# A 31-tap convolution over grid rows: from VectorE taps to TensorE matrices, with relayouts through DRAM

## The chip, the core and the metric

The kernel runs on one core of a Trainium2 chip. The metric is device time of one execution in microseconds. Engines are named as in the profile: PE is TensorE (PEld its weight loads), DVE VectorE, ACT ScalarE, POOL GpSimd, SP the queue that issues most DMAs.

## What is computed

One layer of a hybrid backbone: 1024 latent tokens on a grid of 16 rows of 64 columns, 256 context tokens, width 1024. An input projection gives a DeltaNet head group (queries, keys, values, gates) and a Conformer channel group of 512 channels; both are put together, projected, and followed by a mixture of experts. The change concerns the channel group alone:

```
y = a * sigmoid(b)                    # a, b: 512 columns each of the input projection
y = conv_grid_columns(y, w) + dw_b    # depthwise, 31 taps along the 16 grid rows, zero padding
y = silu(layernorm(y, ln_g, ln_b))    # over the 512 channels
```

For a channel, column and output row `r` the sum is over input rows `r + t - 15`: with 16 rows every output row sees all 16 input rows, each with its own tap.

## The kernel before

The work is emitted through a framework that builds each engine's instruction order at build time: it simulates the program, takes what is ready by the order of the source (and first what stands under `first()`), and puts in the semaphores. At run time each engine and each DMA queue goes through its fixed order and waits where an operand is missing. Tiles live in pools; a pool has a fixed place and size in every partition, pools opened with `side="right"` are stacked from the other end and grow downwards, and a tile laid over one of a closed pool waits for the last reader of that tile (`reuse_waits="tile"`).

The stages that matter here, all on feature-major tiles (128 channels by tokens):

- `cf_project(j, hf)` (lines 368 to 376) projects block `j` of 128 channels for one half of the tokens: 24 matmuls each for b and a in split fp32 (`fm`, L320), tanh on ScalarE (L374), and on VectorE `YG[j] = (tanh + 1) * a` (L376). The missing factor 0.5 is in the tap weights `cfw` (L400). `YG` has two buffers.
- `load_cf` and `load_in` stream the weights: SP loads (L302), ScalarE and GpSimd split into two parts (L293, L294), two buffers each. `mod_block` (L256 to L268) computes modulation vectors from `w_mod`.
- The convolution (loop at L411): ScalarE starts `ycv[:, j]` with the middle tap and the bias (L421), and VectorE adds the other 30 taps, one instruction each (L427), each on the tokens that the shift of `64 * (t - 15)` leaves.
- The layernorm (L458 to L488) in two halves of 512 tokens: column sums on TensorE (`channel_mean`, L462 and L466), copied by ScalarE (L464), subtraction, squares, reciprocal root, product, silu on VectorE and ScalarE (L473 to L487), and a store to `hc_d` in DRAM (L488).
- `qkv_block` projects a block of 128 channels of the heads: `fm` into PSUM tag "a" (four banks), ScalarE copies to `cx` and `cc` (L557, L565), `conv7` on VectorE (L548), transposes (L573), stores to `kv_d` (L584). Four key blocks come first, then the key norms (L662), then value blocks with `prep1` and `base_inverse` (L694 to L736, with DMAs through `wt_d`, `bounce` and `rep`), then query blocks.
- `conv_out(hf)` (L593 on) reads `hc_d` back in tiles `hcs` of 128 tokens (L602), splits them and multiplies with `w_out` (L612), adds `x` (`hx`, L604, L613) and stores to `yo_d`.

The places of the pools in the program of before, in bytes of each partition: `cf` (YG, modulation weights) 27,104 to 76,896; `gbase` 63,968 to 74,400; `cv` (cx 74,400 to 82,648, then cc, ot, sq, ac) 74,400 to 101,152; `ln` (ycv first, 16,384 bytes, then rv, sql and small ones) 101,536 to 124,896; `win` (weights and activations) 124,896 to 229,344. `cf` and `ln` live together; `cv` and `gbase` are opened after both are closed in the source, but run beside the layernorm where nothing lies under them.

Of the kernel before, what the change touches and what calls it, by code (L numbers as in the profile page):

```python
# [8 lines left out]
F32 = mybir.dt.float32  # L9
# [140 lines left out]
def hybrid_kernel(tc, a, out):  # L150
# [19 lines left out]
    def csl(c):  # L170
        return slice(c * 128, (c + 1) * 128)
# [72 lines left out]
    def vcol(n, i=0, k=1):  # L244
        return vec[:, pos[n] + i:pos[n] + i + k]
# [122 lines left out]
    def cf_project(j, hf):  # L368
        wb, wa = wab[j]
        if hf == 0:  # L370
            YG[j] = cfp.tile([128, 1024], F32, name="yg", bufs=2)
        pb = fm(wb, 1 + hf)
        tb = cfp.tile([128, 512], F32, name="tb", bufs=2)
        S.activation(tb, pb, AF.Tanh, scale=0.5)  # L374
        pa = fm(wa, 1 + hf)
        V.scalar_tensor_tensor(YG[j][:, hf * 512:(hf + 1) * 512], tb, 1.0, pa, op0=OP.add, op1=OP.mult)  # L376
# [20 lines left out]
    PE.transpose(pt[:, 0:84], cr, ident[:84, :84])  # L397
    PE.transpose(pt[:, 128:252], fr, ident[:124, :124])
    V.tensor_copy(cnv, pt[:, 0:84])
    V.tensor_scalar(cfw, pt[:, 128:252], 0.5, None, op0=OP.mult)  # L400
    load_x(0, 2)
    stats(0, 2)
    scale_shift('mcx', 'g_mix', 8, 0, 1)
# [1 line left out]
    st_pre.close()  # L405


    st_l = ExitStack()
    lnp = st_l.enter_context(tc.tile_pool(name="ln", bufs=1, side="right", reuse_waits="tile"))
    ycv = lnp.tile([128, 4, 1024], F32, name="ycv")  # L410
    for j in range(4):  # L411
        if j:
            for hf in range(2):
                cf_project(j, hf)
        if j < 3:
            load_cf(j + 1)
        for n in (4 + 2 * j, 5 + 2 * j):
            mod_block(n)
        yg = YG[j]
        yc = ycv[:, j, :]  # L420
        S.activation(yc, yg, AF.Identity, scale=cfw[:, 60 + j:61 + j], bias=vcol('dw_b', j))  # L421
        for t in range(31):
            if t == 15:
                continue
            d = (t - 15) * 64
            lo, hi = max(0, -d), min(1024, 1024 - d)
            V.scalar_tensor_tensor(yc[:, lo:hi], yg[:, lo + d:hi + d], cfw[:, t * 4 + j:t * 4 + j + 1], yc[:, lo:hi],  # L427
                                   op0=OP.mult, op1=OP.add)

    scale_shift('mf', 'g_ffn', 32, 24, 0)  # L430
    gt_d = dp.tile([32, 128], F32, name="gt_d")
# [23 lines left out]
    hc_d = dp.tile([128, 4, 1024], F32, name="hc_d")  # L455


    def channel_mean(get):  # L458

        ps = bank("b")  # L460
        for j in range(4):
            PE.matmul(ps[32 * j:32 * j + 32, :], ones[:, :32], get(j), start=True, stop=True, tile_position=(0, 32 * j))  # L462
        sm = lnp.tile([128, 512], F32, name="sm", tag="rv", bufs=1)
        S.activation(sm, ps, AF.Copy)  # L464
        ps = bank("b")
        PE.matmul(ps, onm, sm, start=True, stop=True)  # L466
        return ps

    for hf in range(2):
        sl = slice(hf * 512, (hf + 1) * 512)  # L470
        pm = channel_mean(lambda j: ycv[:, j, sl])
        for j in range(4):
            V.tensor_sub(ycv[:, j, sl], ycv[:, j, sl], pm)  # L473

        def square(j):
            sq = lnp.tile([128, 512], F32, name="sql", bufs=2)
            S.activation(sq, ycv[:, j, sl], AF.Square)
            return sq

        pv = channel_mean(square)  # L480
        rv = lnp.tile([128, 512], F32, name="rv", bufs=1)
        V.tensor_scalar(rv, pv, EPS, None, op0=OP.add)
        S.activation(rv, rv, AF.Sqrt)
        V.reciprocal(rv, rv)
        for j in range(4):
            V.tensor_mul(ycv[:, j, sl], ycv[:, j, sl], rv)
            S.activation(ycv[:, j, sl], ycv[:, j, sl], AF.Silu, scale=vcol('ln_g', j), bias=vcol('ln_b', j))  # L487
            SY.dma_start(hc_d[:, j, sl], ycv[:, j, sl])  # L488
# [104 lines left out]
    def conv_out(hf):  # L593

        hs_ = slice(hf * 512, (hf + 1) * 512)
        gb = cvp.tile([128, 512], F32, name="gb", tag="sq", bufs=1)
        SY.dma_start(gb, gt_d[4 * hf:4 * hf + 4].rearrange("k p -> (k p)").partition_broadcast(128))
        wt = [load_w(w['w_out'].rearrange("(k p) n -> p k n", p=128)[:, 4 + 2 * i:6 + 2 * i, hs_], 2, gb)
              for i in range(2)]
        for t in range(8):  # L600
            hs = cvp.tile([128, 4, 128], F32, name="hcs", tag="ot", bufs=2)
            SY.dma_start(hs, hc_d[:, :, csl(t)])  # L602
            hx = prp.tile([128, 512], F32, name="hx", tag=("rf", "rb")[t % 2])
            SY.dma_start(hx, x[csl(t), hs_])  # L604
            hr = cvp.tile([128, 2, 4, 128], F32R, name="hcr", tag="ac", bufs=2)
            hch, hcl = split(hs, hr[:, 0], hr[:, 1], (V, G)[t % 2])
            yield
            ps = bank("a")
            for k in range(4):
                wh, wl = wt[k // 2]  # L610
                for i, (l, r) in enumerate(((hch, wh), (hcl, wh), (hch, wl))):
                    PE.matmul(ps, l[:, k, :], r[:, k % 2, :], start=(k == 0 and i == 0), stop=(k == 3 and i == 2))  # L612
            V.tensor_tensor(hx, ps, hx, op=OP.add)  # L613
            SY.dma_start(yo_d[csl(t), hs_], hx)
# [1218 lines left out]
```

## Time and profile before

| | us |
|---|---|
| median of 3 runs | 1735.57 (1733.73 to 1736.39) |
| the profiled execution | 1741.28 |
| its span, first to last instruction | 1739.6 |
| PE busy in the span | 1575.7 |
| DVE busy | 1001.3 |
| ACT busy | 494.5 |
| POOL busy | 537.5 |

A busy share over the span says little, since the stages differ: up to some 563 us the projections, convolutions and preparations run, then the scans, then the experts. An instruction that ends late matters only if another one waits for it; so the views by stage, in order of time and of the waits are read together. The mean granted clock of TensorE over the span was 0.964.

### The profile page before, as it was taken

What the parts mean: (1) busy time and instruction counts of PE and PEld (TensorE: products, weight loads), DVE (VectorE), ACT (ScalarE), POOL (GpSimd) and SP (SyncE); (2) the same over time, 40 slices, a digit from 0 to 9 for tenths busy, and PEclk for the clock granted to TensorE, in tenths of its full rate; (3) what the DMA queues carried; (4) which work ended last, traced back from release to release, by engine and by line L of the source; (5) the groups of instructions that cost most, each with busy time, mean ns of one, the idle gap of its engine ahead of it and who ended that gap; (6) DMA issues with size and microseconds to landing.
All of it is one profiled execution on the core that took longest, in us unless ns stands there. A gap on an engine that the chain in (4) does not pass through costs nothing. (4 is left out here: it accounts for less than half of the span.)

```text
span 1739.6 us, 23353 instructions
## 1 busy us (share of the span) xinstructions
PE 1575.7 (91%) x8348; PEld 924.7 (53%) x8348; DVE 1001.3 (58%) x2236; ACT 494.5 (28%) x1071; POOL 537.5 (31%) x486
## 2 busy tenths in 40 slices
PE   5989998876869899798999999999999999999990
PEld 1557667764647899687544434344444344433440
DVE  2488989889671886878712444444444444443425
ACT  4531266534122212444212121212121111121212
POOL 2321214543212677732011232323232222232212
PEclk8999999998889999899999999999999999999995
DMA  9455123434643334766358999999999999999956
GB/s 318 152 175 176 37 65 94 121 106 124 167 145 127 109 104 154 233 220 218 120 223 304 340 345 342 329 366 335 334 380 381 342 337 331 344 383 370 354 137 232
DMA packets 151112, 412.12 MB, mean 237 GB/s; under 512 B 19383, under 2 KB 66900, under 8 KB 125396
## 3 DMA queue, kind: packets, MB, share of 16 engines
q1 hardware_dynamic: 129994, 334.62, 53.3%
q0 software_dynamic: 18288, 67.05, 15.2%
q10 hardware_dynamic: 2714, 8.95, 1.3%
q8 instruction: 66, 1.08, 0.3%
q14 instruction: 50, 0.41, 0.1%
HBM read 339.48 MB, written 71.43 MB: 236 GB/s over the span
## 5 line engine op out<-in xcount | busy, mean ns | idle before, releaser
L1353 PE MATMUL gu<-wg,hg 128*32 128x512 f32 (+2 forms) x1968 | 463.2, 599 | 0.7 <-ACT hg L1604 0.7
L1629 DVE SCALAR_TENSOR_TENSOR ob<-dn,wc,gt2b 128x512 f32<-128x512 f32 x124 | 93.0, 750 | 366.0 <-PE dn L1373 366.0
L1638 POOL DMA_INDIRECT acc<-ob,ic x89 | 134.6, 1513 | 530.3 <-DVE st L1563 460.1
L1353 PEld LDWEIGHTS gu<-wg,hg 128*32 128x32 f32 (+2 forms) x1968 | 148.4, 137 | 203.2 <-issue 159.2
L1373 PE MATMUL dn<-wd,sg 128*32 128x512 f32 (+2 forms) x984 | 226.8, 597 | 0.5 <-ACT sg L1364 0.5
L1604 ACT ACTIVATE hg<-xt,mf 128x128 f32<-128x128 f32 x248 | 93.4, 456 | 376.4 <-PE xt L1598 375.9
L320 PE MATMUL a<-hTh,whi 128*128 128x512 f32 (+1 forms) x448 | 171.5, 383 | 3.7 <-ACT cx L557 3.7
L320 PE MATMUL a<-hTh,wlo 128*128 128x512 f32 (+1 forms) x448 | 170.3, 380 | 0.0
L320 PE MATMUL a<-hTl,whi 128*128 128x512 f32 (+1 forms) x448 | 170.3, 380 | 0.0
L1373 PEld LDWEIGHTS dn<-wd,sg 128*32 128x32 f32 (+2 forms) x984 | 77.8, 137 | 143.5 <-issue 142.7
L294 POOL TENSOR_TENSOR wlo<-wst,whi 128x512 fp32r<-128x512 f32 x56 | 82.3, 1487 | 214.3 <-ACT whi L293 209.7
L1602 DVE TENSOR_SCALAR hg<-xt,mf 128x128 f32<-128x128 f32 x248 | 84.3, 401 | 50.4 <-DMA acc<-hg 50.4
L427 DVE SCALAR_TENSOR_TENSOR ycv<-yg,cfw,ycv 128x64 f32<-128x64 f32 (+14 forms) x120 | 101.3, 844 | 6.1 <-ACT ycv L421 2.9
L320 PEld LDWEIGHTS a<-hTh,whi 128*128 128x128 f32 x448 | 84.8, 189 | 30.2 <-issue 9.9
L320 PEld LDWEIGHTS a<-hTh,wlo 128*128 128x128 f32 x448 | 85.0, 190 | 18.7 <-issue 3.4
L320 PEld LDWEIGHTS a<-hTl,whi 128*128 128x128 f32 x448 | 84.9, 189 | 18.0 <-issue 3.0
L1588 POOL DMA_INDIRECT xg<-xn_d,ig x62 | 74.1, 1195 | 64.9 <-DVE st L1583 28.3
L1552 DVE TENSOR_TENSOR oh<-posl 128x1024 bf16<-128x1024 f32 (+3 forms) x89 | 77.6, 897 | 0.0
L1598 PE MATMUL xt<-ident,xg 128*128 128x128 f32 x496 | 70.3, 285 | 0.0
L293 ACT ACTIVATE whi<-wst 128x512 fp32r<-128x512 f32 x56 | 33.0, 624 | 107.0 <-PE a L320 66.2
L1358 DVE TENSOR_TENSOR sg<-sg,gu 128x256 f32<-128x256 f32 x62 | 26.1, 421 | 63.4 <-ACT sg L1357 63.4
L1357 ACT ACTIVATE sg<-gu 128x256 f32<-128x256 f32 x62 | 23.8, 384 | 134.9 <-PE gu L1353 134.9
(433 smaller groups left out, 2488.5 us busy)
## 6 DMA issues: line engine op xcount, KB each, us to landing
wg<-exp_w_gate SPq DMA_DIRECT2D x64, 1024.0 KB
wg<-exp_w_up SPq DMA_DIRECT2D x64, 1024.0 KB
wd<-exp_w_down SPq DMA_DIRECT2D x64, 1024.0 KB
wm<-w_mod SPq DMA_DIRECT2D x24, 1024.0 KB
wst<-w_in SPq DMA_DIRECT2D x48, 256.0 KB
kv<-kv_d SPq DMA_DIRECT2D x20, 512.0 KB
rep<-bounce SPq DMA_DIRECT2D x5, 1024.0 KB
eb<-egr_d SPq DMA_DIRECT2D x18, 256.0 KB
```

What stands on the lines that cost most here:

```text
L294: eng.tensor_tensor(lo, st, hi.bitcast(F32), op=OP.subtract)
L320: PE.matmul(ps[:, :n], l[:, k, :], r[:, k, t0:t0 + n], start=(k == 0 and i == 0), stop=(k == 7 and i == 2))
L427: V.scalar_tensor_tensor(yc[:, lo:hi], yg[:, lo + d:hi + d], cfw[:, t * 4 + j:t * 4 + j + 1], yc[:, lo:hi], op0=OP.mult, op1=OP.add)
L1353: PE.matmul(pgu[o:o + n, :].rearrange("p (a f) -> p a f", a=2), lhsT(k, o, n), wts[r][0][:, :, k, :], start=(k == 0), stop=(k == 7), tile_ ...
L1373: PE.matmul(pd[o:o + n, :], aT[:, k, o:o + n], wts[r][1][:, k, hf * 512:(hf + 1) * 512], start=(k == 0), stop=(k == 1), tile_position=(0, ...
L1552: V.tensor_tensor(oh[:, :, o:o + n], N.iol[:, None, p0:p0 + n].to_broadcast([128, 8, n]), N.posr[:, :, r:r + 1].to_broadcast([128, 8, n]), ...
L1588: G.indirect_dma_start(out=xg, out_offset=None, in_=xn_d, in_offset=bass.IndirectOffsetOnAxis(ap=ig, axis=0))
L1598: PE.transpose(pt[:, csl(q)], nth(B['xg'][:, 0:1024], 4 * j + q, 8), ident)
L1602: V.tensor_scalar(hg[:, k, :], pt[:, csl(q)], sc_[:, k:k + 1], sh_[:, k:k + 1], op0=OP.mult, op1=OP.add)
L1604: S.activation(hg[:, k, :], pt[:, csl(q)], AF.Identity, scale=sc_[:, k:k + 1], bias=sh_[:, k:k + 1])
L1629: V.scalar_tensor_tensor(ob[:, hs_], res[hf], B['wc'], N.gt2b[:, hs_], op0=OP.mult, op1=OP.mult)
L1638: G.indirect_dma_start(out=acc_d[turn[0]], out_offset=bass.IndirectOffsetOnAxis(ap=ic[:n], axis=0), in_=B['ob'][o:o + n], in_offset=None, ...
```

## The change

The convolution becomes matrix products. `cfw` is laid out by tap and written to DRAM (`tap_d`). For a group of eight channels, a 128x128 matrix `TM` with eight 16x16 blocks on its diagonal is loaded from it: row `q` and column `n` of a block hold tap `q + n`, so that the product gives the output rows in reversed order. `TM` is cleared once by GpSimd; the blocks of 16 groups are loaded by eight DMAs of 256 runs of 64 bytes for each block `j`.

The activations have to stand with (channel, row) on the partitions and the 64 columns along them. So `YG[j]` is stored to `ycf_d` and read back through `rows8` as `yt` (runs of 256 bytes), 16 matmuls of 64 columns make the products in two PSUM banks, ScalarE copies them to `yr`, `yr` is stored to `ycr_d` through `rows8`, and `ycv[:, j]` is loaded from there. The bias is no longer in `ycv`: its sum over the channels is added to the channel sums (`bsum`), and the subtraction of the mean adds it per channel. `conv_out` loads its `hcs` tiles in two DMAs each, since the rows are reversed. New tiles of pool `ln`: two `TM` of 8,192 bytes, `yt` and `yr` of 4,096; `bsum` in `keep`.

```diff
--- before.py
+++ after.py
@@ -397,7 +397,10 @@
     PE.transpose(pt[:, 0:84], cr, ident[:84, :84])
     PE.transpose(pt[:, 128:252], fr, ident[:124, :124])
     V.tensor_copy(cnv, pt[:, 0:84])
-    V.tensor_scalar(cfw, pt[:, 128:252], 0.5, None, op0=OP.mult)
+    V.tensor_scalar(cfw.rearrange("p (j t) -> p t j", j=4), pt[:, 128:252].rearrange("p (t j) -> p t j", j=4), 0.5,
+                    None, op0=OP.mult)
+    tap_d = dp.tile([512, 31], F32, name="tap_d")
+    SY.dma_start(tap_d.rearrange("(j p) t -> p j t", p=128), cfw.rearrange("p (j t) -> p j t", j=4))
     load_x(0, 2)
     stats(0, 2)
     scale_shift('mcx', 'g_mix', 8, 0, 1)
@@ -405,27 +408,55 @@
     st_pre.close()
 
 
+
     st_l = ExitStack()
     lnp = st_l.enter_context(tc.tile_pool(name="ln", bufs=1, side="right", reuse_waits="tile"))
     ycv = lnp.tile([128, 4, 1024], F32, name="ycv")
+    ycf_d = dp.tile([512, 1024], F32, name="ycf_d")
+    ycr_d = dp.tile([512, 1024], F32, name="ycr_d")
+    TM = [lnp.tile([128, 16, 128], F32, name=f"tm{i}") for i in range(2)]
+    for t in TM:
+        G.memset(t, 0.0)
+
+    def rows8(t, j):
+
+        return bass.AP(tensor=t.tensor, offset=t.offset + j * 128 * 1024, ap=[[64, 128], [8192, 16], [1, 64]])
+
+    def load_taps(j):
+        for c in range(8):
+            SY.dma_start(TM[j % 2][16 * c:16 * c + 16, :, 16 * c:16 * c + 16],
+                         bass.AP(tensor=tap_d.tensor, offset=tap_d.offset + (j * 128 + c) * 31,
+                                 ap=[[1, 16], [248, 16], [1, 16]]))
+
+    def row_conv(j):
+        yt = lnp.tile([128, 16, 64], F32, name="yt", bufs=1)
+        SY.dma_start(yt, rows8(ycf_d, j))
+        yr = lnp.tile([128, 16, 64], F32, name="yr", bufs=1)
+        for hf in range(2):
+            ps = bank("a")
+            for g_ in range(8):
+                PE.matmul(ps[:, 64 * g_:64 * g_ + 64], TM[j % 2][:, 8 * hf + g_, :], yt[:, 8 * hf + g_, :], start=True,
+                          stop=True)
+            S.activation(yr[:, 8 * hf:8 * hf + 8, :].rearrange("p g c -> p (g c)"), ps, AF.Copy)
+        SY.dma_start(rows8(ycr_d, j), yr)
+        SY.dma_start(ycv[:, j, :], ycr_d[csl(j)])
+
+    for j in range(2):
+        load_taps(j)
     for j in range(4):
         if j:
             for hf in range(2):
                 cf_project(j, hf)
+        SY.dma_start(ycf_d[csl(j)], YG[j])
         if j < 3:
             load_cf(j + 1)
         for n in (4 + 2 * j, 5 + 2 * j):
             mod_block(n)
-        yg = YG[j]
-        yc = ycv[:, j, :]
-        S.activation(yc, yg, AF.Identity, scale=cfw[:, 60 + j:61 + j], bias=vcol('dw_b', j))
-        for t in range(31):
-            if t == 15:
-                continue
-            d = (t - 15) * 64
-            lo, hi = max(0, -d), min(1024, 1024 - d)
-            V.scalar_tensor_tensor(yc[:, lo:hi], yg[:, lo + d:hi + d], cfw[:, t * 4 + j:t * 4 + j + 1], yc[:, lo:hi],
-                                   op0=OP.mult, op1=OP.add)
+        if j:
+            row_conv(j - 1)
+            if j < 3:
+                load_taps(j + 1)
+    row_conv(3)
 
     scale_shift('mf', 'g_ffn', 32, 24, 0)
     gt_d = dp.tile([32, 128], F32, name="gt_d")
@@ -455,22 +486,29 @@
     hc_d = dp.tile([128, 4, 1024], F32, name="hc_d")
 
 
-    def channel_mean(get):
+    pt = bank("b")
+    for j in range(4):
+        PE.matmul(pt[32 * j:32 * j + 32, 0:1], ones[:, :32], vcol('dw_b', j), start=True, stop=True,
+                  tile_position=(0, 32 * j))
+    bsum = keep.tile([128, 1], F32, name="bsum")
+    V.tensor_copy(bsum, pt[:, 0:1])
+
+    def channel_mean(get, bias=0.0):
 
         ps = bank("b")
         for j in range(4):
             PE.matmul(ps[32 * j:32 * j + 32, :], ones[:, :32], get(j), start=True, stop=True, tile_position=(0, 32 * j))
         sm = lnp.tile([128, 512], F32, name="sm", tag="rv", bufs=1)
-        S.activation(sm, ps, AF.Copy)
+        S.activation(sm, ps, AF.Identity, bias=bias)
         ps = bank("b")
         PE.matmul(ps, onm, sm, start=True, stop=True)
         return ps
 
     for hf in range(2):
         sl = slice(hf * 512, (hf + 1) * 512)
-        pm = channel_mean(lambda j: ycv[:, j, sl])
+        pm = channel_mean(lambda j: ycv[:, j, sl], bsum)
         for j in range(4):
-            V.tensor_sub(ycv[:, j, sl], ycv[:, j, sl], pm)
+            V.scalar_tensor_tensor(ycv[:, j, sl], ycv[:, j, sl], vcol('dw_b', j), pm, op0=OP.add, op1=OP.subtract)
 
         def square(j):
             sq = lnp.tile([128, 512], F32, name="sql", bufs=2)
@@ -599,7 +637,9 @@
               for i in range(2)]
         for t in range(8):
             hs = cvp.tile([128, 4, 128], F32, name="hcs", tag="ot", bufs=2)
-            SY.dma_start(hs, hc_d[:, :, csl(t)])
+            for i in range(2):
+                r_ = 15 - 2 * t - i
+                SY.dma_start(hs[:, :, 64 * i:64 * i + 64], hc_d[:, :, 64 * r_:64 * r_ + 64])
             hx = prp.tile([128, 512], F32, name="hx", tag=("rf", "rb")[t % 2])
             SY.dma_start(hx, x[csl(t), hs_])
             hr = cvp.tile([128, 2, 4, 128], F32R, name="hcr", tag="ac", bufs=2)
```

## Rows read from the trace of the kernel before

**Rows 1.** The page's head: the span and its instructions.

```profile
span 1739.6 us, 23353 instructions
```

**Rows 2.** Busy us (count) by stage: PE, PEld, DVE, ACT, POOL; PEclk, DMA, GB/s.

```profile
...
96.00:189.00 93.00, 85.73 (x422) 60.10 (x414) 84.26 (x122) 23.34 (x36) 17.45 (x12) 0.98 0.50 169
189.00:206.00 17.00, 17.00 (x91) 13.44 (x89) 16.30 (x22) 1.53 (x3) 0.22 (x1) 1.00 0.02 2
206.00:219.00 13.00, 11.31 (x41) 6.43 (x40) 12.24 (x39) 5.86 (x12) 6.13 (x16) 1.00 0.15 40
219.00:262.00 43.00, 43.00 (x204) 30.23 (x203) 36.71 (x44) 28.56 (x42) 6.00 (x10) 1.00 0.22 66
262.00:301.00 39.00, 33.99 (x192) 28.59 (x192) 35.02 (x46) 23.02 (x40) 15.90 (x19) 1.00 0.35 105
301.00:405.00 104.00, 82.04 (x416) 68.04 (x414) 90.20 (x135) 51.49 (x85) 48.73 (x44) 0.92 0.38 105
405.00:460.00 55.00, 41.21 (x141) 29.35 (x141) 47.50 (x84) 20.03 (x30) 16.39 (x16) 0.84 0.59 154
460.00:505.00 45.00, 25.53 (x99) 19.02 (x100) 30.54 (x59) 8.35 (x13) 9.43 (x7) 0.81 0.59 162
```

**Rows 3.** Groups by line, 0 to 420 us: count, busy us, mean ns, idle before.

```profile
...
L427 DVE SCALAR_TENSOR_TENSOR ycv<-yg,cfw,ycv 128x64 f32<-128x64 f32 (+14 forms) x120 | 101.3, 844 | 6.1 <-ACT ycv L421 2.9
```

**Rows 4.** VectorE in order of time: start us, us, instruction and its count.

```profile
...
184.34 0.67 DVE L376 SCALAR_TENSOR_TENSOR yg<-tb,a 128x512 f32<-128x512 f32 x1
...
194.00 18.21 DVE L427 SCALAR_TENSOR_TENSOR ycv<-yg,cfw,ycv 128x768 f32<-128x768 f32 x19
...
218.97 1.28 DVE L548 SCALAR_TENSOR_TENSOR kf<-cx,cnv,kf 128x1024 f32<-128x1024 f32 x1
...
301.32 1.02 DVE L662 TENSOR_SCALAR ssk<-ssk 128x40 f32<-128x40 f32 x1
```

**Rows 5.** ScalarE in order of time.

```profile
...
206.12 0.58 ACT L557 ACTIVATE cx<-a 128x512 f32<-128x512 f32 x1
213.34 0.60 ACT L464 ACTIVATE sm<-b 128x512 f32<-128x512 f32 x1 [6.64 <-PE b L462]
...
260.62 2.94 ACT L487 ACTIVATE ycv<-ycv,vec 128x512 f32<-128x512 f32 x4
```

**Rows 6.** L548 alone, by stage: DVE busy (count), PEclk, DMA share, GB/s.

```profile
...
219.00:262.00 43.00, 20.74 (x24) 1.00 0.22 66
262.00:301.00 39.00, 28.12 (x34) 1.00 0.35 105
```

**Rows 7.** TensorE's matmuls in order of time.

```profile
...
181.87 0.39 PE L320 MATMUL a<-hTl,whi 128*128 128x512 f32 x1
182.10 0.39 PE L320 MATMUL a<-hTh,wlo 128*128 128x512 f32 x1
...
295.43 1.06 PE L698 MATMUL b<-kf 128*128 128x128 f32 x8
```

**Rows 8.** Waits (us, times, longest), 212 to 301 us; last row 301 to 563.

```profile
...
POOL cc L563 <- DVE kf L548: 18.9, 3, 7.4
...
DVE tm L730 <- DMA rep<-bounce: 23.3, 5, 8.9
```

**Rows 9.** SP's issues in order of time.

```profile
...
312.23 0.34 SPq L709 DMA_DIRECT2D wt_d<-wt  x1
314.26 0.79 SPq L714 DMA_DIRECT2D bounce<-wt_d  x1
...
402.72 0.60 SPq L602 DMA_DIRECT2D hcs<-hc_d  x1
```

**Rows 10.** DMA busy share, 402.7 to 407.7 us in 40 slices.

```profile
DMA  0000000000027889998410000000499830336969
```

**Rows 11.** The same, 314.2 to 316.5 us, and its packets.

```profile
DMA  0000000000090000000000000000332235557773
...
DMA packets 501, 0.05 MB, mean 21 GB/s; under 512 B 500, under 2 KB 500, under 8 KB 500
```

## The prediction

> **What bounds the kernel now.** I read the page first: one core, a span of 1739.6 us [rows 1], and the profiled execution took 1741.28 us, so 1.7 us lie around the span. It is 5.7 us above the median of the runs (1735.57); I add up changes of the span and put them on the median. The change touches nothing after 563 us but the alignment of what follows, so the second view is the busy time by stage up to there [rows 2]. The reader is to see three things. From 96 to 189 us, while the channel group's projections run, TensorE is busy 85.7 of 93 us and VectorE 84.3: both are nearly full, so taking work from VectorE alone can't shorten this stage by more than TensorE's 7.3 idle us. From 189 to 262 us TensorE is busy 71.3 of 73. From 262 to 505 us neither is full (TensorE 182.8, VectorE 203.3 of 243), VectorE the fuller one: there they wait for each other and for DMAs.
>
> The third view is the line of the taps: 120 instructions, 101.3 us of VectorE [rows 3]. The fourth is VectorE's order of time [rows 4]: the last half of YG[3] is written at 184.3 to 185.0, the taps of block 3 run until 212.2, and the first tap of the key blocks' conv7 follows at 218.97. ScalarE's order [rows 5] shows that the first projection of key block 0 is copied to cx at 206.12 and that the layernorm runs from 213.34 (first sum copied) to 263.6 (last silu): beside the key blocks, not ahead of them. Of VectorE's time from 219 to 262 the conv7 had 20.7 us [rows 6]. So only 189 to 219 us is a place where the taps hold VectorE while other work of the next stage is there, and that is the most the removal can give at once.
>
> **The change, part by part.**
> Removed: 120 taps and 4 ScalarE starts, 101.3 us of VectorE [rows 3]. Most of it lies beside TensorE's projections, which stay; I count no gain for it up to 189 us.
>
> Added on TensorE: per block 16 fp32 matmuls of 128x128 on 64 columns, 32 records. The nearest row is L698, fp32 with the same weights and 128 columns: 8 records in 1.06 us, 0.13 each [rows 7]. That bounds a block at 4.2 us; half of it, 2.1, is the other bound, if columns alone counted. I take 4, since each record brings its own weights there as here. Three blocks' matmuls come before the end of block 3's projection: +12 us, of which I let 4 go into the 7.3 idle us: **+8** at that point (bounds -1 and +12.6; by the next paragraph up to +27).
>
> Added waits: the order of every queue is written at the build. Where a DMA lands later than that order assumed, the engine stands still: five times VectorE waited for rep, 4.7 us each [rows 8]. The convolution's matmuls wait for yt the same way, and behind them stand the projections on TensorE; three such waits would be 14 us. I count none in the sum, all in the range.
>
> Added DMAs, and the chain after YG[3]: store to ycf_d, load yt, matmuls, copy, store yr, load ycv, and only then the layernorm's last sums. A plain store of 256 KB landed within 2.03 us (wt_d issued 312.23, its reader issued 314.26) [rows 9]; 512 KB I take as 3.5. A load of 256 KB in 512-byte rows (hcs, issued 402.72 [rows 9]) began to move 1.4 us after issue and was done 1.2 us later, ten slices of 0.125 us [rows 10]: 512 packets over 16 engines, 38 ns each. 500 packets of 64 bytes were through in 0.7 us, 12 slices of 0.0575 us [rows 11]: 22 ns each. yt and yr have 2048 packets of 256 bytes, 128 an engine: 2.8 to 4.8 us; I take 4, and with 1.4 to start and about 1 to land 6.5 each. Matmuls and the copy are 4.8, the load of ycv 4. Chain: 3.5 + 6.5 + 4.8 + 6.5 + 4 = **26 us** (bounds 18, with the small packets' rate and half the fixed parts, and 36, with each 256-byte packet at twice its price). The layernorm's last sums can then start at 185 + 8 + 26 = 219 us, against some 212 before: 7 us late. The tap loads (32 DMAs of 256 rows of 64 bytes) and TM's two memsets run while the queue has little else to do; at 0.8 us an issue, as bounce took [rows 9], 16 of them hold SP for 13 us before block 0's yt. I cost them at nothing, covered by block 0's early YG and by the 27 us until block 1's; without that cover they would add up to 13 us there.
>
> **What I think decides: the room the new tiles take.** TM (2 x 8 KB), yt and yr (4 KB each) make the pool `ln` 24,576 bytes larger in each partition. In the program of before `cv` ends 384 bytes below `ln`, so that cx, cc, ot, sq and ac share no byte with ycv. `ln` grows downwards, from 101,536 to 76,960, and `cv` (from 74,400, 32 more for bsum) then lies under ycv and TM. So cx can't be written before ycv is released, after its last reader, the last store to hc_d. That reuse waits for readers the trace shows already with cx's and cc's own buffers: GpSimd waited 18.9 us for conv7 to let go of cc [rows 8]. The key blocks now start behind the layernorm instead of beside it.
>
> Its price: the layernorm took 50.2 us (213.34 to 263.6 [rows 5]); without the conv7's 20.7 [rows 6] it is 29.5. It ends at 219 + 29.5 = 248.5, its last store has landed at 250.5, and the first copy to cx comes then, against 206.12. Four projections fit into the four PSUM banks of tag "a" meanwhile (both halves and the context of key block 0, one half of block 1); after that TensorE has nothing to do. From 250.5 it still owes half a block, a context part and two blocks: matmuls of 512 columns follow each other at 0.23 us [rows 7], 24 make 5.5 us, the 256-column ones I take at half, so 5.5 + 2.8 + 2 x 13.8 = 36; some 5 for transposes, and 3 for a lowered clock behind the gap (from 460 to 505 us, where TensorE stood still for 19.5 of 45 us, the granted clock was 0.81 on the mean, between the levels of 2.4 and 1.2 GHz [rows 2]). Key block 3 is projected at 294.5, its conv7, silu and sums take some 13.5 more (an instruction of L548 takes 48.9 / 58 = 0.84 us by [rows 6]; a block's twelve are 10.1, most of them behind the last projection, the rest is estimated), and the key norms come at 308 against 301.3 [rows 4]: 7 late. By then VectorE had, before, done most of value block 0 too: of L548's 58 instructions in 219 to 301 us [rows 6] 48 belong to the keys, ten of twelve to value block 0, 8.4 us. So VectorE is 15.4 us behind. From 301 to 460 us it idled 21.3 us [rows 2]; I let a third of that, 7, take up delay (between none and all of it, nearer none because most of it waits for DMAs whose own start is late then), and **+8** stay.
>
> Moved: each hcs load becomes two DMAs of 256-byte rows. Sixteen become 32, each one more issue of 0.6 us [rows 9] and 1.0 us more of packets; the stores and hx loads queue behind them on SP. A quarter of 16 x 1.0 on the path: **+4** (bounds 0, hidden, and 16). The bias moves into the layernorm's subtraction: same instruction count, nothing. Sum: +12; 1735.6 + 12 = 1747.6, **1748 us**.
>
> The Trainium skill (DMA: Bandwidth & Descriptors, Specifications) speaks against this change: transfers under 512 bytes are read-modified-written. No row of before shows a store of 256-byte rows, so nothing here agrees or disagrees yet; by the rule the sum would be the first step of the heavier rival below, 1758, and by the rows it is 1748.
>
> **The rivals.**
> *Faster: VectorE's relief arrives.* Place: 206 to 219 us. If the room doesn't bind and cx is free before the layernorm is through, conv7 can start 2.4 us after the first copy, at 208.5 + 8 instead of 218.97, and what VectorE did between 212.2 and 218.97 besides the layernorm's subtraction (4 of 6.8 us, estimated) is made earlier: -2.5 - 4, about -7; if TensorE's own +8 is hidden too, -15. That gives 1728 (1721 to 1732). For it: VectorE is the fuller engine from 262 on. Against: the bytes above. It decides if the first copy to cx comes ahead of the layernorm's last silu.
> *Absorbed.* VectorE's 35.8 idle us from 301 to 505 [rows 2] take the whole delay: 1732 to 1739. For it: five waits for rep lengthen by themselves when work ahead is late. Against: rep's own load waits for the work that is late.
> *Heavier.* Each 256-byte packet costs double the larger bound, 76 ns: yt and yr take 128 x 0.076 = 9.7 us to move, 5 to 6 more each, so 1748 + 10 = 1758. If three of the fixed-order waits (4.7 each) come true as well, 1758 + 14 = 1772 (whole rival: 1757 to 1780, the doubling alone 0.10, both 0.08). For it: rep. Against: 64-byte packets moved at 22 ns [rows 11]. The Trainium skill's rule on small transfers, named above, would put this rival on top.
>
> **How the numbers follow.** Forecast 0.50 (own range 1739 to 1757), faster 0.19, absorbed 0.13, heavier 0.18. The time is the forecast's. The range of 1727 to 1768 leaves out half of the faster rival and a third of the heavier one, together 0.16. About 0.2% (3.5 us) is what runs of this kernel can tell from no change: faster than that 0.19, within 0.13, slower 0.68.
>
> **What would show it.** In the profile after: VectorE's busy time down by some 100 us; L557's first copy behind the last hc_d store, near 250; a gap of 20 us or more on TensorE between block 3's projection and that copy; conv matmuls at about 0.13 us a record; yt and yr at 6 to 7 us from issue to use; key norms a few us late. I am wrong if cx is copied at 210 to 220, or if the gap is there and the stage's end at 563 doesn't move.

## The result: slower by 2.7%

The changed kernel takes 1781.84 us (median of four runs, 1779.81 to 1789.05) against 1735.98 for the kernel before on the same chip: a ratio of 1.0274, 95% interval 1.0243 to 1.0305. The forecast was 1748 us with a range up to 1768. The sign was right and so was the place; the price was a quarter of what came: +12 us was forecast, and a ratio of 1.0274 is +47.6 on 1736. The profiled execution took 1789.05 us with a span of 1787.3, 47.7 more than before [rows 1].

The page after: the span, each engine's busy time, and the DMA packets.

```profile
span 1787.3 us, 23622 instructions
...
PE 1607.0 (90%) x8484; PEld 952.6 (53%) x8484; DVE 910.5 (51%) x2117; ACT 495.0 (28%) x1075; POOL 539.7 (30%) x488
...
DMA packets 186457, 421.12 MB, mean 236 GB/s; under 512 B 61895, under 2 KB 101220, under 8 KB 160740
```

VectorE lost 90.8 us of work (1001.3 before), TensorE gained 31, and packets under 512 bytes went from 19,383 to 61,895. The windows after, by the same stages as [rows 2] (busy us and instructions of each engine, granted TensorE clock, DMA share, GB/s):

```profile
core 0: us, PE busy (x) PEld busy (x) DVE busy (x) ACT busy (x) POOL busy (x), PEclk, DMA share, GB/s
96.00:189.00 93.00, 90.54 (x442) 69.36 (x436) 6.59 (x22) 17.89 (x29) 10.11 (x8) 0.94 0.69 203
189.00:206.00 17.00, 13.82 (x102) 9.07 (x101) 8.55 (x34) 3.94 (x7) 5.55 (x9) 0.89 0.66 174
206.00:219.00 13.00, 13.00 (x50) 10.33 (x50) 0.13 (x1) 1.71 (x3) 1.27 (x1) 0.75 0.57 159
219.00:262.00 43.00, 32.70 (x112) 16.32 (x110) 14.82 (x17) 19.62 (x26) 2.52 (x2) 0.78 0.12 38
262.00:301.00 39.00, 29.70 (x155) 25.38 (x156) 33.49 (x39) 20.75 (x35) 11.30 (x22) 0.85 0.20 61
```

Up to 189 us VectorE is nearly empty now (6.6 us against 84.3), and TensorE fuller than before. From 219 to 301 us, where TensorE was busy 77 of 82 us before, it is busy 62.4, at a mean granted clock of 0.78 and 0.85: it waits. For what, ScalarE's and TensorE's order of time show (start, duration, engine, line, what, idle time before and what ended it):

```profile
223.80 0.69 ACT L502 ACTIVATE sm<-b,bsum 128x512 f32<-128x512 f32 x1 [12.91 <-PE b L500]
...
240.62 2.93 ACT L525 ACTIVATE ycv<-ycv,vec 128x512 f32<-128x512 f32 x4 [2.85 <-DVE ycv L524]
243.46 0.67 ACT L502 ACTIVATE sm<-b,bsum 128x512 f32<-128x512 f32 x1
...
264.26 2.93 ACT L525 ACTIVATE ycv<-ycv,vec 128x512 f32<-128x512 f32 x4 [2.85 <-DVE ycv L524]
269.55 1.08 ACT L595 ACTIVATE cx<-a 128x512 f32<-128x512 f32 x2 [2.36 <-DMA hc_d<-ycv]
```

```profile
270.20 0.79 PE L320 MATMUL a<-hTh,whi 128*128 128x512 f32 x1 [11.54 <-ACT cx L595]
270.79 0.63 PE L320 MATMUL a<-hTl,whi 128*128 128x512 f32 x1
...
274.54 0.39 PE L320 MATMUL a<-hTh,wlo 128*128 128x512 f32 x1
```

The first copy to cx comes at 269.55 us (206.12 in [rows 5]), 2.36 us behind the layernorm's last silu, released by its last store to hc_d. TensorE stands still for 11.54 us ahead of it, and the matmuls behind the gap take 0.63 us, the lower level of the clock, until 274 us; then they take 0.39. The layernorm itself runs from 223.80 to 264.26 + 2.93 = 267.2: 43.4 us. Its lateness begins in SyncE's queue:

```profile
189.93 0.34 SPq L450 DMA_DIRECT2D ycf_d<-yg  x1
...
198.37 0.37 SPq L433 DMA_DIRECT2D yt<-ycf_d  x1
...
210.40 0.37 SPq L441 DMA_DIRECT2D ycr_d<-yr  x1
...
214.32 0.34 SPq L442 DMA_DIRECT2D ycv<-ycr_d  x1
```

YG[3] is stored at 189.93, but yt is loaded only at 198.37: there is one yt buffer, and block 2's matmuls are ordered behind the modulation blocks. TensorE then waits 3.18 us for it, at a fallen clock:

```profile
202.68 7.06 PE L438 MATMUL a<-yt,tm 128*128 128x64 f32 x32 [3.18 <-DMA yt<-ycf_d]
```

Behind the stage the loads of hcs are the next wait (who waited for the tile, us, times):

```profile
who waited for it (us, times):
...
  ACT hcr L293: 34.3, 8
```

34.3 us in 8 waits, where the kernel before had 14.8 in 5.

### The profile page after: what moved, and what is told of

Its sections match the earlier page's. It is cut to its first block, busy times and chain, and to the rows that moved or that the text cites. A ratio compares the mean times of both kernels' runs of the same rounds, so it can differ in the third digit from the quotient of the medians.

```text
span 1787.3 us, 23622 instructions
## 1 busy us (share of the span) xinstructions
PE 1607.0 (90%) x8484; PEld 952.6 (53%) x8484; DVE 910.5 (51%) x2117; ACT 495.0 (28%) x1075; POOL 539.7 (30%) x488
## 5 line engine op out<-in xcount | busy, mean ns | idle before, releaser
L652 PE MATMUL a<-whi,hcr 128*128 128x512 f32 x128 | 47.8, 452 | 17.0 <-ACT hcr L293 8.1
L1638 PEld LDWEIGHTS xt<-ident,xg 128*128 128x128 f32 x496 | 60.3, 194 | 1.4 <-issue 1.4
```

Source lines behind the costliest of these rows:

```text
L1638: PE.transpose(pt[:, csl(q)], nth(B['xg'][:, 0:1024], 4 * j + q, 8), ident)
```

## The experiments

The theories at the start: 1, the room orders the key blocks behind the layernorm; 2, the relayouts, tap loads and added matmuls cost the time; 3, the second load of hcs does. All runs read the same marks (us in the profiled execution; "sums" is the first copy of the layernorm's sums, "out" the first and last matmul of this group's output projection; the ratio is to the kernel before, with its interval; e10 and e12 were run once, the other times are medians):

| kernel | last YG[3] | sums | first cx | last silu | key norms | out | first gather | time, us | ratio |
|---|---|---|---|---|---|---|---|---|---|
| kernel before | 184.3 | 213.3 | 206.1 | 262.8 | 301.3 | 418.2 to 532.4 | 871.0 | 1735.98 | 1 |
| changed kernel | 189.2 | 223.8 | 269.6 | 266.4 | 334.5 | 457.3 to 587.2 | 919.2 | 1781.84 | 1.0274 (1.0243 to 1.0305) |
| e1 | 185.3 | 214.3 | 255.1 | 251.9 | 320.2 | 454.3 to 561.3 | 892.1 | 1764.16 | 1.0159 (1.0138 to 1.0180) |
| e2 | 188.8 | 223.4 | 263.9 | 263.2 | 332.1 | 454.9 to 584.8 | 916.4 | 1782.95 | 1.0253 (1.0233 to 1.0272) |
| e3 | 188.4 | 222.4 | 266.2 | 263.0 | 331.2 | 463.9 to 571.4 | 903.0 | 1807.91 | - |
| e4 | 184.0 | 218.6 | 259.7 | 256.5 | 324.6 | 446.9 to 575.2 | 907.1 | 1778.5 | 1.0244 (1.0222 to 1.0266) |
| e5 | 187.4 | 220.6 | 214.7 | 271.1 | 314.8 | 436.8 to 559.1 | 888.7 | 1759.66 | 1.0124 (1.0107 to 1.0142) |
| e6 | 187.8 | 222.3 | 268.0 | 264.9 | 333.0 | 466.4 to 572.0 | 904.1 | 1774.06 | 1.0193 (1.0172 to 1.0215) |
| e7 | 185.2 | 219.7 | 213.7 | 270.2 | 315.7 | 445.0 to 556.3 | 890.2 | 1757.98 | 1.0109 (1.0093 to 1.0126) |
| e8 | 190.4 | 216.2 | 210.0 | 268.2 | 310.3 | 441.7 to 550.0 | 882.7 | 1753.65 | 1.0078 (1.0049 to 1.0108) |
| e9 | 189.6 | 223.5 | 217.5 | 274.0 | 319.3 | 448.9 to 558.7 | 889.8 | 1763.3 | 1.0158 (1.0115 to 1.0201) |
| e10 | 182.4 | 208.2 | 203.9 | 259.9 | 301.8 | 431.0 to 541.9 | 871.5 | 1742.31 | - |
| e11 | 185.6 | 213.4 | 207.7 | 264.9 | 307.7 | 438.0 to 546.2 | 883.6 | 1751.95 | 1.0079 (1.0055 to 1.0103) |
| e12 | 174.0 | 182.7 | 190.3 | 228.9 | 285.4 | 406.8 to 520.0 | 856.8 | 1833.91 | - |

e3_one_hcs, e10_flat_rows and e12_no_taps compute something else, the routing behind them changes, and only marks up to the first gather compare. The first gather also leaves out what the expert stage adds by chance. The marks are those of one profiled execution each. YG[0] already came at 71.3 to 74.8 us, ahead of any change, and from YG[0] to YG[3] the same code took 111.8 us in e4 and 117.3 in the changed kernel: a difference of some 5 us between two profiles says nothing by itself. The profiled execution of the kernel before lay 5.3 us above its median, that of the changed kernel 7.2, the others within 3.8 of theirs.

**e1: the room alone.** To the kernel before:

```diff
     ycv = lnp.tile([128, 4, 1024], F32, name="ycv")
+    room = lnp.tile([128, 6144], F32, name="room")
+    G.memset(room[:, 0:8], 0.0)
```

> The kernel before with its taps on VectorE, and in the layernorm's pool one more tile of 24,576 bytes behind ycv, of which eight columns are set to zero and nothing is read. Theory 1 (room: ycv now lies under the key blocks' tiles, so that they start behind the layernorm's last store): the first copy to cx comes at 213 + 43 + 2 = about 258 us instead of 206, the key norms some 20 to 25 us late, and the time is 1755 to 1765 us. Theory 2 (the relayouts, the tap loads and the added matmuls cost the time): nothing moves, 1733 to 1739 us.

Measured: 1.0159, +27.6 us. ScalarE's order of time:

```profile
214.32 0.60 ACT L466 ACTIVATE sm<-b 128x512 f32<-128x512 f32 x1 [7.11 <-PE b L464]
...
249.79 2.93 ACT L489 ACTIVATE ycv<-ycv,vec 128x512 f32<-128x512 f32 x4 [2.85 <-DVE ycv L488]
...
255.11 1.09 ACT L559 ACTIVATE cx<-a 128x512 f32<-128x512 f32 x2 [2.38 <-DMA hc_d<-ycv]
```

With the taps still on VectorE, no relayout and no added matmul, an idle tile sends the key blocks behind the layernorm and costs 27.6 us. Theory 1 holds, theory 2 can't be the whole. The key norms come 18.9 us late, a little under the 20 to 25 expected. The layernorm alone takes 38.4 us here.

**e2: other addresses, e5: a pool of its own.** To the changed kernel; e2 only allocates TM, yr and yt ahead of ycv in the pool `ln`, e5 gives them the same addresses in another pool:

```diff
+    st_t = ExitStack()
+    tmp_ = st_t.enter_context(tc.tile_pool(name="taps", side="right", ...))
-    TM = [lnp.tile(...) ...]          # yt and yr likewise
+    TM = [tmp_.tile(...) ...]
...
     row_conv(3)
+    st_t.close()
```

> The changed kernel with the tap matrices, yr and yt allocated ahead of ycv, so that ycv is back at 101,536 and the key blocks' tiles lie under tiles that are dead after the convolution. Theory 1: the first copy to cx comes at 207 to 216 us, TensorE has no gap of 11 us before it, and 30 to 40 of the 46 us go: 1742 to 1752 us. Theory 2: the time stays within 5 us of the changed kernel's, 1777 to 1787 us.

> The changed kernel with the tap matrices, yt and yr in a pool of their own below the layernorm's, closed right behind the last block's convolution; the addresses are those of the run in which these tiles only came first. Theory 1b (a tile's room is handed on at the close of its pool, not at its last reader, so that in that run the key blocks were still ordered behind the layernorm although they shared no byte with ycv): the first copy to cx comes at 206 to 216 us, TensorE has no gap before it, and the 25.7 us that the room alone cost go: 1748 to 1758 us. Rival (relayout chain and added matmuls hold the key blocks back anyway): 1772 to 1784 us.

Measured: e2 1.0253, inside the interval of the changed kernel; e5 1.0124, 26 us less than the changed kernel (1759.66, 1.7 above the bound given). In e2 ycv shares no byte with cx, and yet:

```profile
261.08 2.93 ACT L527 ACTIVATE ycv<-ycv,vec 128x512 f32<-128x512 f32 x4 [2.85 <-DVE ycv L526]
263.92 1.05 ACT L597 ACTIVATE cx<-a 128x512 f32<-128x512 f32 x2
```

```profile
L598 ACT ACTIVATE cx<-a x24: 571/584/602, 214.7 to 502.1; 128x512 f32<-128x512 f32 x24
```

In e2 the copy follows the last silu with no wait between (no store is waited for now): the order written at the build still has cx behind the layernorm. The tile under cx there, a TM, had its last reader at 208.2 us at the latest (TensorE, L440). In e5 the first copy is at 214.7. My theory for e2, that bytes decide, fell; what decides is when the pool that held the bytes is closed. `ln` closes behind the layernorm, so nothing of `cv` that lies in its range is ordered ahead of that, whether the tile there is dead or not. So what I wrote of pools at the start, that a tile laid over one of a closed pool waits for the last reader of that tile, is not the whole: the order of the build waits for the close as well.

**e4: the layernorm's halves.** The second half gets yt's buffer for sm and rv:

```diff
-        pm = channel_mean(lambda j: ycv[:, j, sl], bsum)
+        tag = ("rv", "yt")[hf]
+        pm = channel_mean(lambda j: ycv[:, j, sl], bsum, tag)
...
```

> The changed kernel with a buffer of its own for sm and rv in the layernorm's second half (the room of yt, which is dead by then). Theory 1a (the 43.4 us of the layernorm come from its halves sharing one buffer for sm and rv): the second half's first sm is copied ahead of the first half's last silu, the layernorm takes 28 to 34 us, the first copy to cx comes at 256 to 260 us and the time is 1768 to 1774 us. Rival (the halves follow each other for another reason, or the delay is made up later): within 4 us of the changed kernel, 1778 to 1786 us.

```profile
218.58 0.69 ACT L502 ACTIVATE sm<-b,bsum 128x512 f32<-128x512 f32 x1 [12.96 <-PE b L500]
...
231.17 0.67 ACT L502 ACTIVATE sm<-b,bsum 128x512 f32<-128x512 f32 x1
237.43 2.93 ACT L526 ACTIVATE ycv<-ycv,vec 128x512 f32<-128x512 f32 x4
...
254.37 2.93 ACT L526 ACTIVATE ycv<-ycv,vec 128x512 f32<-128x512 f32 x4 [2.84 <-DVE ycv L525]
```

The second half starts ahead of the first one's silu (231.17 against 237.43), as theory 1a said, but the layernorm still takes 38.7 us, and the ratio is 1.0244, 5 us less with intervals that overlap. The shared buffer is a small part of the 43.4. The rest is a chain: in 223.8 to 267.2 us of the changed kernel ScalarE is busy 22.6 us, VectorE 19.6, TensorE 27.9, none of them full, and by the idle times above each waits for the other:

```profile
223.80:267.20 43.40, 27.89 (x93) 13.26 (x93) 19.62 (x23) 22.55 (x30) 2.52 (x2) 0.72 0.15 49
```

The clock has a part in it: the two products with onm (L504) take 1.05 and 1.02 us in the first half of the tokens and 2.07 each in the second, where TensorE had run out of projections.

**e3 and e6: one load of hcs.** e3 loads the tile as before and leaves the rows reversed; e6 loads tile 7 - t and swaps its two rows where it is split:

```diff
-            for i in range(2):
-                r_ = 15 - 2 * t - i
-                SY.dma_start(hs[:, :, 64 * i:64 * i + 64], hc_d[:, :, 64 * r_:64 * r_ + 64])
+            SY.dma_start(hs, hc_d[:, :, csl(7 - t)])
...
-            hch, hcl = split(hs, hr[:, 0], hr[:, 1], (V, G)[t % 2])
+            split(hs.rearrange("p k (i c) -> p k i c", i=2)[:, :, ::-1, :], ...)
```

> The changed kernel with one load of hcs for each tile, as before; the rows of the grid stay in the order in which the convolution left them (this reversal is left out). The prediction's price of the split was 4 us: 1778 us. Theory 3 (the split is dear: the output projection of this group grew from 114 to 130 us beside it): 12 to 16 us less, 1766 to 1770 us.

> The changed kernel with one load of hcs for each tile in 512-byte rows, as before; the two grid rows of a tile are swapped where hcs is split into its high and low parts, by the order in which these instructions read it. Theory 3 (the split into two loads of 256-byte rows is dear): the output projection of this group takes 110 to 118 us instead of 130, and the time is 1764 to 1770 us. By the prediction's price of 4: 1776 to 1780 us.

Measured: e6 1.0193, 14 us less; the first gather 15.1 us earlier, in e3 16.2 (e3's total of 1807.91 us is that of another routing and says nothing). From the first to the last matmul of the output projection it is 105.6 us in e6, 107.5 in e3, 129.9 in the changed kernel; ScalarE waits 3.0 us for hcs in e6. Theory 3 holds. The price is not the split's own, though: with the pool of its own the same edit (e5 to e7) gives 2.6 us, with intervals that overlap. The output projection gets 11.0 us shorter there too (122.3 to 111.3), but it starts 8.2 us later.

**e7 and e8: both edits, then two buffers for yt.**

```diff
-        yt = tmp_.tile([128, 16, 64], F32, name="yt", bufs=1)
+        yt = tmp_.tile([128, 16, 64], F32, name="yt", bufs=2)
...
-        yr = tmp_.tile([128, 16, 64], F32, name="yr", bufs=1)
+        yr = yt
```

> The two edits together: a pool of their own for the tap matrices, yt and yr, and one load of hcs for each tile. If room and split are the whole loss, 1733 to 1744 us; if the relayout chain and the added matmuls cost something of their own, more: each us that the layernorm's last sums start behind those of the kernel before, up to 10, so up to 1750 us.

> The two edits together, and yr written into yt's own room, so that yt has two buffers in the same bytes: block 3's yt can be loaded before block 2's matmuls are through, which held its issue from 190 to 198 us. If the chain behind the last block sets the layernorm's start: its last sums 5 to 8 us earlier and 2 to 8 us less than the run without this edit. If what the key blocks do beside the layernorm sets the end of the stage: the same within 3 us.

Measured: 1.0109 and 1.0078, still 18.9 and 13.5 us above before; e7's 1757.98 is above the 1750 that I gave as the most. Room and split are 29 of the 47.6 us, not all. From e7 to e8 it is 5.4 us (intervals that overlap), the first gather 7.5 earlier. In e8 the sums come 25.8 us after YG[3], in e7 34.5.

**e9: the matmuls twice.** To e8:

```diff
-            for g_ in range(8):
+            for g_ in [g_ for g_ in range(8) for _ in range(2)]:
```

> The run with two buffers for yt, each of its 64 convolution matmuls issued twice, the second over the first. A block's 32 records took 3.8 us there. Theory 4 (what is left of the loss is the work that the convolution adds to TensorE, which is full from 96 to 262 us): the 15 us of added records come out nearly whole, 10 to 15 us later, 1764 to 1769 us, and the key norms 10 to 15 us later. Rival (the chain of relayouts behind the last block is what is left): only that block's 3.8 us, 1756 to 1758 us.

Measured: 1.0158, 13.9 us more than e8 by the ratios (9.7 by the medians), key norms 9.0 us later, so the medians and the key norms lie just under the bounds. A block's records, in e9 and in e10 (below):

```profile
125.46 7.33 PE L440 MATMUL a<-yt,tm 128*128 128x64 f32 x64 [0.56 <-DMA yt<-ycf_d]
```

```profile
125.72 3.68 PE L440 MATMUL a<-yt,tm 128*128 128x64 f32 x32
```

From YG[0] to YG[3], with two blocks' matmuls between them, it is 118.3 us in e9, 110.1 in e10 and 102.5 in e12, which has none; the granted clock from 120 to 150 us was 1.00 in all three. Two blocks at 3.7 us are 7.4, and the steps are 8.2 and 7.6. What is added on TensorE there comes out whole; theory 4 holds for the matmuls.

**e10: plain rows.** To e8, rows of 4 KB in place of 256-byte pieces:

```diff
-        return bass.AP(tensor=t.tensor, ..., ap=[[64, 128], [8192, 16], [1, 64]])
+        return bass.AP(tensor=t.tensor, ..., ap=[[1024, 128], [64, 16], [1, 64]])
```

> The run with two buffers for yt, the loads of yt and the stores of yr in plain rows of 4 KB in place of 256-byte pieces: the relayout is left out, so the matmuls mix other rows, the routing may change, and the times are read up to the first gather. By the prediction's prices (6.5 us each from issue to use, of which 4 is the moving of the packets) the layernorm's last sums start 2 to 5 us earlier; by the heavier rival (76 ns a packet) 10 to 12 us earlier. If theory 4 holds, the first gather comes at most 5 us earlier.

One run: the first gather at 871.5, 11.2 us ahead of e8's. That is more than I gave theory 4, but not all of it is the price of small pieces. YG[3] is 8.0 us earlier; 2.5 of them were there at YG[0], and of the other 5.5 most go with a lower clock that small pieces need not bring. From YG[0] to YG[3] it is 115.6 us in e8 and 110.1 in e10, but 112.1 in e7, which has e8's 256-byte pieces. From 120 to 150 us the granted clock (third number from the end) was 0.89 in e8, 1.00 in e7 and 1.00 in e10:

```profile
120.00:150.00 30.00, 28.45 (x142) 20.89 (x141) 2.26 (x7) 4.14 (x7) 2.51 (x2) 0.89 0.84 248
```

```profile
120.00:150.00 30.00, 28.65 (x157) 21.28 (x157) 2.27 (x7) 5.77 (x10) 4.41 (x4) 1.00 0.79 227
```

```profile
120.00:150.00 30.00, 29.29 (x160) 22.39 (x153) 1.77 (x7) 5.03 (x9) 5.01 (x4) 1.00 0.70 226
```

That leaves some 2 us for the pieces ahead of YG[3]. Behind YG[3] the sums come after 25.8 us in both, yet the pieces show: from the issue of yt's last load to that of ycv's it is 15.0 us in e8 (194.12 to 209.08) and 12.0 in e10 (188.47 to 200.50). Most of what e10 won there it lost in SyncE's queue, where yt's load was issued 5.3 us behind the store of YG[3] instead of 3.0. The one run of e10 is 4.0 us below the fastest of e8's four (1746.30 to 1755.92), so the price of the small pieces is 11 us at most and not known better.

**e11: block 3 alone on TensorE.** To the kernel before; YG[3] is written with its rows reversed, its taps are reversed, and its convolution goes through a pool of its own:

```diff
+        if j == 3:
+            SY.dma_start(ycf_d, yg)
+            row_conv()
+            st_t.close()
+            S.activation(ycv[:, 3, :], ycv[:, 3, :], AF.Identity, bias=vcol('dw_b', 3))
+            break
```

> The kernel before with the last of the four channel blocks alone convolved on TensorE, in a pool of its own, with the grid rows of that block reversed ahead of the convolution and its taps reversed, so that hcs is loaded as before. VectorE loses 25 us of taps behind 185 us, TensorE gets 3.8 us. If freeing VectorE from 185 to 212 us is worth what the faster rival gave it: 1726 to 1733 us. If TensorE sets this stage and the chain of relayouts (26 us) only takes the place of the taps (27 us): 1736 to 1744 us.

Measured: 1.0079, +13.7 us; neither guess. VectorE is free from 185 us, but the first sums come at 213.4, as before: the chain of relayouts, 27.8 us behind YG[3], took the place of the taps, as the second guess had it. The loss is on TensorE. The matmuls wait for yt, the projections stand behind them, and the clock falls. In e11:

```profile
189.00:206.00 17.00, 14.24 (x61) 11.94 (x62) 4.68 (x30) 1.79 (x3) 2.01 (x14) 0.70 0.40 92
```

```profile
193.69 7.09 PE L440 MATMUL a<-yt,tm 128*128 128x64 f32 x32 [1.37 <-DMA yt<-ycf_d]
200.54 0.77 PE L320 MATMUL a<-hTh,whi 128*128 128x512 f32 x1
```

In the kernel before:

```profile
189.26 0.50 PE L320 MATMUL a<-hTh,whi 128*128 128x512 f32 x1
```

TensorE is busy 14.24 of 17 us at 0.70, where it had 17 at 1.00 [rows 2], and the block's records take 7.1 us instead of 3.7 at the upper level. The key blocks' projections begin at 200.54 us, 11.3 later than before. This is the fixed-order wait that the prediction kept out of its sum. The first copy to cx does not show it (207.7 against 206.1); the key norms come 6.4 us late and the first gather 12.6; that the 11.3 us make the whole 13.7 is argued from their place and size, not shown.

**e12: no taps at all.** In the kernel before the 120 taps on VectorE are left out; the middle tap and the bias stay.

> The kernel before with the 120 tap instructions left out (the middle tap and the bias stay), which changes the routing; times are read up to the first gather. It bounds what taking 101 us from VectorE can give if nothing replaces it. By the prediction: nothing up to 189 us, the layernorm's last sums right behind YG[3] at 187 to 190 instead of 212, the first copy to cx within 3 us of 206, and the first gather 7 to 15 us earlier than 871. If VectorE were the bound: 40 us or more.

One run: YG[3] at 174.0, the sums at 182.7, the first gather at 856.8, 14.2 us earlier. That is inside the bounds given, but not for the reason given: 8.9 of the 14 us are won between YG[0] and YG[3], where the prediction counted nothing, and the first copy to cx comes at 190.3, not within 3 us of 206. TensorE's row from 96 to 189 us, 85.73 busy in [rows 2]:

```profile
96.00:189.00 93.00, 92.98 (x454) 64.92 (x452) 12.97 (x48) 25.16 (x41) 17.16 (x26) 1.00 0.48 165
```

The first gather by steps, one profile each: 871.0 before; 856.8 without taps; 871.5 with the matmuls and plain relayouts in their place (e10); 882.7 with 256-byte pieces (e8); 890.2 with one yt (e7); 904.1 with the tiles in `ln` (e6); 919.2 with two loads of hcs, the changed kernel. By these marks, what the change saved, 14 us, its matmuls and plain DMAs took back before anything else was paid; steps of 5 us among them can be chance.

## Why the prediction was wrong

*The step that failed* is the price of the room. The mechanism was right (key blocks behind the layernorm, the first copy to cx released by its last store, a gap on TensorE, though of 11.54 us and not of 20), if its reason was too narrow: e2 shows that not only ycv's bytes hold cx back, but the whole range of `ln` until it closes. But the layernorm alone was put at 50.2 - 20.7 = 29.5 us and took 43.4; e1, with nothing else changed, shows 38.4. By the prediction's own terms the room alone is worth 2 to 3 us (cx at 213.34 + 29.5 + 2 = 244.8, key norms at 302.3, then 8.4 - 7 more); e1 measured 27.6. Subtracting VectorE's conv7 assumed that VectorE sets its length. It is a chain of short instructions on three engines, and without the conv7 beside it its waits stay. That alone makes the first copy to cx 14 us later than forecast. The key norms came 26.5 us later than forecast: 4.8 by the first copied sum (223.8 instead of 219), 13.9 by the layernorm, 0.4 by its last store, 7.4 behind the first copy to cx. With 10.1 more for hcs that is 36.6, against the 35.6 us missed.

The other terms, in the prediction's order:

- *Taps gone, nothing gained up to 189 us*: wrong in size. e12 has YG[3] 10.3 us earlier, 8.9 of it behind YG[0]. TensorE's idle 7.3 us before were three waits for ScalarE's ms (L259), behind a start of ycv (L421) that waited for VectorE's yg; in e12 they are gone. The bound of 7.3 us was there in the text, and the sum used 4 of it, to hide added matmuls.
- *TensorE +12, YG[3] +8*: a block's 32 records took 3.7 to 3.8 us at the upper level of the clock (4 forecast), 6.4 and 7.1 in two blocks of the changed kernel where it was lower. Only two blocks' matmuls stood ahead of YG[3], not three (64 records up to 189 us). YG[3] came 4.9 us late; in e4 and e7, with the same code up to there and no fall of the clock from 120 to 150 us, it came 0.3 early and 0.9 late. e9 shows that this work comes out whole.
- *No fixed-order wait*: one of 3.2 us for yt, with the lower clock behind it (0.75 from 206 to 219 us). The range held it, the sum did not; in e11 a wait of 1.4 us and a block at the lower clock put the projections back by 11.3.
- *The chain of 26 us*: its parts add up to 25.3, and with two yt buffers it took 25.8 (e8, e10). Part of that is luck: in e8 the store of yr took 4.0 us to the next issue instead of 6.5, and from the issue of ycv's load to the first copied sum it was 7.1 instead of 4. The one-buffer wait from 189.93 to 198.37 was missed; the last sums ran at 222.7 instead of 219.
- *256-byte packets, 22 to 38 ns*: too dear. The last store of yr moved 219 GB/s over 16 engines, 18.7 ns a packet, 2.4 us instead of 4; yt took 4.3 us from issue to use and yr 3.9 (198.37 to 202.68, 210.40 to 214.32), not the 6 to 7 given as a sign. What the pieces cost ahead of YG[3], some 2 us by e7 and e10, no term held.
- *From the first copy to the key norms, 57.5 us*: 64.9, so the key norms came at 334.5 instead of 308; the clock behind the gap cost about 1.7 us (nine matmuls at 0.43 instead of 0.23 us pitch), less than the 3 allowed for it; where the rest went stays open. In e1 it was 65.1.
- *VectorE 8.4 us further behind, 7 absorbed*: right at the value blocks. The first value block's product with rk came 42.5 us late, 9.3 more than the key norms; at the last it was 36.6, 5.9 less. It did not stay so to the stage's end: in e1 and e5 to e9 the time from the key norms to the last projection is 274.6 to 277.3 us against 268.0. To the first gather it is 570.5 to 574.5 in them against 569.7.
- *hcs, +4 with a bound of 16*: 14.1 us in this kernel (e6); 2.6 with the pool of its own (e5 to e7), not clear of noise. The bound was right; what decides between its ends is not shown.

Of the rivals, the faster one failed at the point named for it (cx not ahead of the last silu), absorption failed as well, and the heavier one had the time nearest, though also too low, and not for its reason: a 256-byte packet took 18.7 ns and not 76, and the small pieces cost at most 11 of the 47.6 us (e10).

The Trainium skill (DMA: Bandwidth & Descriptors, Specifications) has transfers under 512 bytes read-modified-written. The trace agrees in direction: the stores of yr in 256-byte pieces moved 219 GB/s with all engines busy, in rows of 4 KB 378. The 512-byte rows of [rows 10] moved 256 to 358 GB/s, 311 on the mean, in the 0.44 us in which the engines were full, so the same bytes took 1.4 to 1.7 times as long in 256-byte pieces. No run shows the read-modify-write itself, and a store is not needed for the loss: in e8 the load of yt alone moved 219 GB/s as well. The packets of the two stores of yr:

```profile
DMA packets 1286, 0.33 MB, mean 219 GB/s; under 512 B 1286, under 2 KB 1286, under 8 KB 1286
```

```profile
DMA packets 133, 0.49 MB, mean 378 GB/s; under 512 B 13, under 2 KB 13, under 8 KB 133
```

A load and a store of such pieces together lose less. From 198.37 to 203.37 us of the changed kernel block 3's yt and block 2's yr moved beside each other, at some 290 GB/s:

```profile
GB/s 0 0 0 0 0 0 0 0 92 176 174 176 160 127 158 152 170 197 260 291 295 283 295 287 289 291 289 283 250 264 287 293 287 289 285 293 287 293 295 285
DMA packets 3849, 0.98 MB, mean 196 GB/s; under 512 B 3848, under 2 KB 3849, under 8 KB 3849
```

Open: why the key norms come some 5 us later behind the first copy to cx in e5, e7 to e9 and e11 than before (100.0 to 102 against 95.2 us); why the split's price depends so much on the pool; why the clock fell between 120 and 150 us in some profiles and not in others; and whether a relayout without DRAM would turn the sign. No version here beats the kernel before; the best, e8, is at 1.0078 (1.0049 to 1.0108).

## What to carry to other kernels

Before moving work off an engine, ask which engine the stage waits for: here VectorE's 101 us were worth 14 us in the one run without them, and TensorE, which took the work over, was the one that was full. Count a new tile's bytes as an order: it holds whatever comes to lie in its pool's range until that pool closes, so short-lived tiles belong in a pool of their own that closes behind their last reader. Take the length of a stage that is a chain between engines from its own rows, not by subtracting the work that ran beside it. And before a difference between two profiles is given to an edit, look for a third with the same code in that stretch: here it took most of the 5.5 us away.

## What the runs showed that I had not expected

- In e11 TensorE stood still for 2.8 of 17 us, 1.4 of them for yt, at a mean granted clock of 0.70; the projections behind that began 11.3 us late.
- 256-byte packets moved at 18.7 ns each, below the 22 ns read for 64-byte packets [rows 11] and half of the 38 read for 512-byte rows [rows 10]: both prices came from one short transfer, with its start and its end in them.
- The second load of hcs cost 14.1 us in one kernel and 2.6, not clear of noise, in another that differs only in the pool of four tiles.
